# Moving the start addresses of the wide products' operands to multiples of 256 bytes in a partition

## The chip, the core and the metric

The kernel runs on one core of a Trainium2 chip. The metric is the device time of one execution in microseconds. Before the change the median of 3 runs is 2291.79 us (2289.28 to 2292.4). In the text TensorE is PE, its weight loads are PEld, VectorE is DVE, ScalarE is ACT, GpSimd is POOL and SyncE is SP.

## What is computed

A network of four layers on 256 tokens of 1024 features. Each layer is a half-weighted SwiGLU feed-forward block, a mixer, and a second feed-forward block, each added to the running `x` after an RMS norm:

```python
for i in range(DEPTH):
    x = x + 0.5 * _swiglu(_rms(x, norm_g[i, 0]), ffn_w_gate[i, 0], ffn_w_up[i, 0], ffn_w_down[i, 0])
    h = _rms(x, norm_g[i, 1])
    y = mixer[i](h)            # S5, HGRN2, gated delta net, MoBA attention
    x = x + y
    x = x + 0.5 * _swiglu(_rms(x, norm_g[i, 2]), ffn_w_gate[i, 1], ffn_w_up[i, 1], ffn_w_down[i, 1])
return _rms(x, final_norm_g)
```

A feed-forward block has two matrices of 1024x2816 and one of 2816x1024 in float32. There are eight such blocks, and the mixers have their own projections of 1024 to 2048, 4096, 6176 and 3072 columns and back.

## The kernel before

**Products in three passes.** All weights are float32 in HBM. `Weights._load` brings 128x1024 elements (512 KB) into a `raw` tile; `pump` makes `hi`, a rounded copy in the type fp32r, on ACT (L88), and `lo`, the rest, on DVE (L91; on POOL for every second unit of the delta net). The activations are split in the same way into a hi and a lo half, which stand side by side in one tile. A product is then hi x hi, hi x lo and lo x hi, three matmuls of type fp32r.

**The wide products** are in `Model.wide` (L347 to L349). The weights stream past (the moving operand, 128x512, from `hi` or `lo`), and a 128x128 piece of the activations is loaded into the array (the stationary operand). The tiles that give the stationary operand are `xhl` (the normed `x`, for up and gate projections and mixers), `hhl` (the hidden layer of a feed-forward block, for its down projection), `yhl`, `o` and `go` (the outputs of the mixers):

```python
ah, al = [a[:, k + j, m, t * 128:t * 128 + 128] for m in range(2)]
mm(p, ah, hi[:, j], start=first and j == 0, stop=False)
mm(p, ah, lo[:, j], start=False, stop=False)
mm(p, al, hi[:, j], start=False, stop=last and j == n - 1)
```

Each matmul has a weight load of its own. There are 2464 such triples, 7392 matmuls.

**The column products** are in `mm3` (L315 to L317), for those projections of the mixers whose result is wanted turned. The roles are changed there: 128x128 pieces of `hi` and `lo` are loaded, and 256 columns of `xhl` stream. There are 520 triples, 1560 matmuls.

**What sets the order.** Every engine's program is written out in full by the kernel's Python code, in the order of the blocks in `PARTS`; `take` and `pump` keep four units of weights split ahead of PE and four `raw` tiles loaded ahead. SP issues the loads of the weights.

**Where tiles start.** Tiles of a pool lie one behind the other in a partition, each begun at a multiple of 32 bytes, and the pools lie in the order in which `Model.__init__` opens them: `const`, `xp`, `small`, `work`, `raw`, `split`, then the pools of the single blocks. Within the tiles all operands of the two products are taken at steps of 512 bytes, so an operand's start, modulo 256, is that of its tile. Worked out from the tiles' sizes, the starts modulo 256 bytes are, before and after the change:

| operand | before | after | matmuls |
| --- | --- | --- | --- |
| wide, moving: `hi`, `lo` | 224 | 0 | 7392 |
| wide, stationary: `xhl` | 64 | 0 | 4704 |
| wide, stationary: `hhl` of the 8 feed-forward blocks in order | 128, 224, 192, 224, 64, 224, 224, 224 | 192, then 0 seven times | 8 x 264 |
| wide, stationary: `yhl` (S5), `go` (delta net), `o` (MoBA) | 224 | 0 | 192, 192, 96 |
| wide, stationary: `o` (HGRN2) | 192 | 0 | 96 |
| columns, moving: `xhl` | 64 | 0 | 1560 |
| columns, stationary: `hi`, `lo` | 224 | 0 | 1560 |

`raw` goes from 224 to 0 too. Before, `gains` (448 bytes), `hg_b` (132), `s5place` (32), `gd_w` (516) and `half_r` (8) are the tiles with sizes that are no multiple of 256 ahead of operands in their pools.

Of the kernel before, what the change touches and what calls it, by code (L numbers as in the profile page):

```python
# [9 lines left out]
F32 = mybir.dt.float32  # L10
# [17 lines left out]
def as_ap(ap, offset, dims):  # L28
    return bass.AP(tensor=ap.tensor, offset=ap.offset + offset, ap=dims)


class Weights:
# [6 lines left out]
    def __init__(self, nc, raw, split):  # L39
        self.nc, self.raw, self.split = nc, raw, split  # L40
        self.blocks, self.units = [], []
        self.loaded = self.ready = self.taken = 0
        self.tiles, self.parts = {}, {}
        self.aside = set()
# [59 lines left out]
class Model:  # L104
    def __init__(self, ctx, tc, I, out, parts):
        self.tc, self.nc, self.I, self.out = tc, tc.nc, I, out
        nc = self.nc
        self.const = ctx.enter_context(tc.tile_pool(name="const", bufs=1))
        self.xp = ctx.enter_context(tc.tile_pool(name="xp", bufs=1))
        self.small = ctx.enter_context(tc.tile_pool(name="small", bufs=2))  # L110
        self.work = ctx.enter_context(tc.tile_pool(name="work", bufs=2))
        raw = ctx.enter_context(tc.tile_pool(name="raw", bufs=Weights.RAW))
        split = ctx.enter_context(tc.tile_pool(name="split", bufs=Weights.HL))
        self.acc = ctx.enter_context(tc.tile_pool(name="acc", bufs=4, space=PSUM))
        self.dram = ctx.enter_context(tc.tile_pool(name="dram", bufs=1, space=bass.MemoryType.DRAM))
        self.w = Weights(nc, raw, split)
        self.parts = parts
        self.beside = []
        for p in parts:
            getattr(self, "plan_" + p[0])(*p[1:])  # L120
        with self.banks():
            self.start()
        self.prep = self.ahead = None
        self.bias = self.moba_bias if any(a[0] == "moba" for a in parts) else None
        with ExitStack() as early:
            for n, p in enumerate(parts):
                nxt = parts[n + 1] if n + 1 < len(parts) else None
                if n == 0 and any(a[0] == "s5" for a in parts):
                    self.s5_gain = self.gain_of([a for a in parts if a[0] == "s5"][0])
                    self.s5_pool = early.enter_context(tc.tile_pool(name="s5prep", bufs=1))  # L130
                    self.s5_u = self.s5_pool.tile([128, KT, 2, 8, 16], F32, name="s5u", tag="s5u")
                    self.prep = self.s5_prep(self.s5_pool)
                self.next_gain = self.gain_of(nxt)
                self.for_s5 = nxt is not None and nxt[0] == "s5"
                if nxt is not None and nxt[0] in ("hgrn", "gdn"):
                    made = early.enter_context(ExitStack())
                    pool = made.enter_context(tc.tile_pool(name="made", bufs=1))
                    self.ahead = lambda: getattr(self, nxt[0] + "_consts")(pool, *nxt[1:])
                aux = early.enter_context(ExitStack())
                aux.enter_context(self.banks(1 if p[0] == "gdn" else 4))  # L140
                self.due = p[0] in ("hgrn", "gdn", "moba")
                if p[0] != "s5":
                    self.r_col = self.norm_col()
                if p[0] == "s5":
                    self.settle(self.prep)
                    self.prep = None
                if nxt is None:
                    self.end = aux.enter_context(self.tc.tile_pool(name="last", bufs=1))
                    self.fin = self.end.tile([128, D], F32, name="fin")
                    nc.scalar.dma_start(self.fin, as_ap(I["final_norm_g"], 0, [[0, 128], [1, D]]))  # L150
                getattr(self, p[0])(*p[1:])
                aux.close()
                if p[0] in ("hgrn", "gdn") and n:
                    made.close()
                if p[0] == "s5":
                    early.close()
# [14 lines left out]
    def start(self):  # L171
        nc, I = self.nc, self.I
        c = self.const
        x = I["x"]

        self.x = self.xp.tile([128, 2, D], F32, name="x")
        rows = self.work.tile([128, 128], F32, name="rows", bufs=1)
        nc.sync.dma_start(rows[:96], as_ap(I["norm_g"], 0, [[128, 96], [1, 128]]))
        for c0 in range(0, D, 512):
            nc.sync.dma_start(self.x[:, :, c0:c0 + 512], as_ap(x, c0, [[D, 128], [128 * D, 2], [1, 512]]))  # L180
        nc.scalar.dma_start(rows[96:104], as_ap(I["final_norm_g"], 0, [[128, 8], [1, 128]]))
        nc.scalar.dma_start(rows[104:112], as_ap(I["s5_d"], 0, [[128, 8], [1, 128]]))
        self.ident = c.tile([128, 128], F32, name="ident")
        nc.gpsimd.memset(self.ident, 0.0)
        nc.gpsimd.affine_select(out=self.ident, in_=self.ident, compare_op=OP.not_equal, fill=1.0,
                                base=0, pattern=[[-1, 128]], channel_multiplier=1)
        self.zero = c.tile([128, 512], mybir.dt.bfloat16, name="zero")
        nc.vector.memset(self.zero, 0.0)
        self.gains = c.tile([128, 112], F32, name="gains")
        p = self.aux.tile([128, 512], F32, name="aux")  # L190
        nc.tensor.transpose(p[:, :112], rows[:112], self.ident[:112, :112])
        nc.scalar.copy(self.gains, p[:, :112])
        self.next_gain = self.gain_of(self.parts[0])
        self.r_row = self.xp.tile([128, L], F32, name="r_row")
        self.for_s5 = False
        self.begin_x()
        self.w.pump(1, self.tc.keep_in_program_order)
        for cc in range(2):
            for t in range(2):
                self.turn_x(t, cc)  # L200
            self.w.pump(2 + cc, self.tc.keep_in_program_order)
        for cc in range(2):
            for t in range(2):
                self.square_x(t, cc)
# [383 lines left out]
    def s5_prep(self, pool):  # L588


        nc, I = self.nc, self.I
# [16 lines left out]
        p = self.aux.tile([128, 512], F32, name="aux")  # L608
# [8 lines left out]
        for src, first, second, signs in ((b_in, b1, b2, (1, 1, -1, 1)), (c_in, c1, c2, (1, -1, -1, -1))):  # L617
            for h0 in (0, 8):
                p = self.aux.tile([128, 512], F32, name="aux")
# [93 lines left out]
        split = lambda a: a.rearrange("p g (t h) -> p g t h", h=16)  # L713
# [5 lines left out]
        for sign, base in ((1, 0), (-1, 7)):  # L719
            nc.gpsimd.affine_select(out=self.s5_at, in_=self.s5_at, compare_op=OP.is_ge, fill=0.0, base=base,  # L720
                                    pattern=[[128 * sign, 2], [0, 4], [-8 * sign, 32]], channel_multiplier=sign)
        self.s5_place = pool.tile([128, 8], F32, name="s5place")
        v.tensor_reduce(self.s5_place, self.ident.rearrange("p (a t) -> p t a", t=8), op=OP.add, axis=mybir.AxisListType.X)
        for j in range(8):
            r = slice(8 * j, 8 * j + 8)
# [17 lines left out]
            p = self.aux.tile([128, 512], F32, name="aux")  # L743
# [13 lines left out]
            for h, eb in zip(rs, ebs):  # L757
                p = self.aux.tile([128, 512], F32, name="aux")
# [265 lines left out]
    def hgrn_consts(self, pool, i):  # L1024

        nc = self.nc
# [4 lines left out]
        nc.gpsimd.dma_start(rows[32:33], as_ap(self.I["hg_norm_g"], 0, [[128, 1], [1, 128]]))  # L1031
        p = self.aux.tile([128, 512], F32, name="aux")
        nc.tensor.transpose(p[:, :33], rows[:33], self.ident[:33, :33])
        b = pool.tile([128, 33], F32, name="hg_b")
        nc.vector.tensor_copy(b, p[:, :33])
        c = pool.tile([128, 3, 8], F32, name="hg_c")
        m = pool.tile([128, 3, 8], F32, name="hg_m")
        nc.vector.tensor_tensor(m[:, 0], b[:, 0:8], b[:, 8:16], op=OP.max)
# [228 lines left out]
    def gdn_consts(self, pool, i):  # L1267
        nc, I = self.nc, self.I
# [4 lines left out]
        p = self.aux.tile([128, 512], F32, name="aux")  # L1273
        nc.tensor.transpose(p[:, :128], rows[:, 0], self.ident)
        nc.tensor.transpose(p[:, 128:129], rows[:1, 1], self.ident[:1, :1])
        self.gd_w = pool.tile([128, 129], F32, name="gd_w")
        nc.vector.tensor_copy(self.gd_w, p[:, :129])
        self.gd_ab = pool.tile([128, 2, 16], F32, name="gd_ab")
        nc.gpsimd.dma_start(self.gd_ab[:, 0], as_ap(I["gdn_a_log"], 0, [[0, 128], [1, 16]]))
        nc.gpsimd.dma_start(self.gd_ab[:, 1], as_ap(I["gdn_dt_bias"], 0, [[0, 128], [1, 16]]))  # L1280
# [20 lines left out]
        for n in range(5):  # L1301
            a = pool.tile([128, 2, 32], I32, name="gd_a")
            b = pool.tile([128, 3, 32], F32, name="gd_b")
# [8 lines left out]
        b = pool.tile([128, 2, 32], F32, name="gd_c")  # L1312
# [13 lines left out]
    def gdn(self, i):  # L1326
        nc = self.nc
        F16 = mybir.dt.float16
        mm = nc.tensor.matmul
        with ExitStack() as ctx:  # L1330
            pool = ctx.enter_context(self.tc.tile_pool(name="gdn", bufs=1))
# [115 lines left out]

                self.proj_cols(4, v_done)

            half_r = pool.tile([128, 2], F32, name="half_r")  # L1450
            nc.vector.tensor_scalar(half_r, self.r_col, 0.5, None, op0=OP.mult)

            def gate(z):
# [371 lines left out]
```

## Time and profile before

| what | value |
| --- | --- |
| median of 3 runs | 2291.79 us |
| the profiled execution | 2291.63 us |
| its span, first to last instruction | 2289.8 us |
| granted TensorE clock, mean | 0.983 |
| PE busy | 2177.5 us (95%) |
| PEld busy | 1774.8 us (78%) |
| DVE busy | 1460.9 us (64%) |
| ACT busy | 1159.5 us (51%) |
| POOL busy | 286.8 us (13%) |
| HBM read | 375.65 MB, 169 GB/s with the writes, over the span |

A busy PE is not a PE at its peak: matmuls overlap, and a matmul of 0.39 us may be followed by the next after 0.23 us. What such a stream costs is therefore read from the distance between starts, or from a stretch's length over the number of matmuls in it, and not from the mean duration. The chain of work that ended last tells which engine's work the end of the program hung on, and for how much of the span.

### The profile page before, as it was taken

What the parts mean: (1) busy time and instruction counts of PE and PEld (TensorE: products, weight loads), DVE (VectorE), ACT (ScalarE), POOL (GpSimd) and SP (SyncE); (2) the same over time, 40 slices, a digit from 0 to 9 for tenths busy, and PEclk for the clock granted to TensorE, in tenths of its full rate; (3) what the DMA queues carried; (4) which work ended last, traced back from release to release, by engine and by line L of the source; (5) the groups of instructions that cost most, each with busy time, mean ns of one, the idle gap of its engine ahead of it and who ended that gap; (6) DMA issues with size and microseconds to landing.
All of it is one profiled execution on the core that took longest, in us unless ns stands there. A gap on an engine that the chain in (4) does not pass through costs nothing.

```text
span 2289.8 us, 30309 instructions
## 1 busy us (share of the span) xinstructions
PE 2177.5 (95%) x11480; PEld 1774.8 (78%) x11480; DVE 1460.9 (64%) x2412; ACT 1159.5 (51%) x1876; POOL 286.8 (13%) x305
## 2 busy tenths in 40 slices
PE   8979788999999999999999888899999999999998
PEld 6767566888888887887888766777788888898886
DVE  7886664556555866556555788977655555666555
ACT  6434344445444755445444567765544444545443
POOL 0597600000000000001000322222000000000000
PEclk9999989999999999999999999999999999999999
DMA  8655966655555644555654532333555655655553
GB/s 251 192 190 200 225 180 158 197 177 191 179 177 178 186 146 150 182 175 175 185 183 161 171 102 86 99 111 114 181 181 169 200 177 173 204 166 175 183 169 108
DMA packets 317906, 389.63 MB, mean 170 GB/s; under 512 B 14192, under 2 KB 247856, under 8 KB 316736
## 3 DMA queue, kind: packets, MB, share of 16 engines
q1 hardware_dynamic: 314768, 383.92, 53.9%
q10 hardware_dynamic: 2800, 3.68, 0.9%
q8 instruction: 90, 1.47, 0.3%
q14 instruction: 56, 0.46, 0.1%
q0 software_dynamic: 192, 0.10, 0.0%
HBM read 375.65 MB, written 12.01 MB: 169 GB/s over the span
## 4 chain that ended last, share of the span: by engine, by line
PE 81%; DVE 9%; ACT 3%; DMA 3%; POOL 2%; issue 1%; SPq 0%; ACTq 0%; DVEq 0%; POOLq 0%
PE acc L348 23%; PE acc L349 23%; PE acc L347 23%; DVE lo L91 2%; PE acc L316 2%; PE acc L315 2%; PE acc L317 2%; PE aux L439 2%; DVE cy L1395 1%; DMA raw<-in_ffn_w_up_dram 1%; ACT hi L88 1%; PE aux L230 1%; DMA tab<-s_k 1%; POOL s5e L734 1%; POOL s5e L733 1%
## 5 line engine op out<-in xcount | busy, mean ns | idle before, releaser
L91 DVE TENSOR_TENSOR lo<-raw,hi 128x1024 fp32r<-128x1024 f32 x648 | 809.8, 1251 | 614.1 <-ACT hi L88 613.1
L88 ACT CAST hi<-raw 128x1024 fp32r<-128x1024 f32 x681 | 712.5, 1048 | 734.2 <-PE acc L349 680.9
L347 PE MATMUL acc<-hi,xhl 128*128 128x512 f32 x1568 | 635.0, 405 | 10.4 <-ACT hi L88 9.6
L348 PE MATMUL acc<-lo,xhl 128*128 128x512 f32 x1568 | 627.9, 400 | 2.4 <-DVE lo L91 2.3
L349 PE MATMUL acc<-hi,xhl 128*128 128x512 f32 x1568 | 626.4, 400 | 0.0
L347 PEld LDWEIGHTS acc<-hi,xhl 128*128 128x128 f32 x1568 | 298.2, 190 | 81.0 <-ACT hi L88 10.5
L349 PEld LDWEIGHTS acc<-hi,xhl 128*128 128x128 f32 x1568 | 297.9, 190 | 73.9 <-issue 2.7
L348 PEld LDWEIGHTS acc<-lo,xhl 128*128 128x128 f32 x1568 | 298.2, 190 | 72.4 <-DVE lo L91 4.9
L349 PE MATMUL acc<-hi,hhl 128*128 128x512 f32 x704 | 278.0, 395 | 0.0
L347 PE MATMUL acc<-hi,hhl 128*128 128x512 f32 x704 | 277.9, 395 | 0.0
L348 PE MATMUL acc<-lo,hhl 128*128 128x512 f32 x704 | 277.0, 393 | 0.0
L348 PEld LDWEIGHTS acc<-lo,hhl 128*128 128x128 f32 x704 | 133.0, 189 | 29.1
L347 PEld LDWEIGHTS acc<-hi,hhl 128*128 128x128 f32 x704 | 132.9, 189 | 28.8
L349 PEld LDWEIGHTS acc<-hi,hhl 128*128 128x128 f32 x704 | 132.8, 189 | 28.7
L317 PE MATMUL acc<-xhl,lo 128*128 128x256 f32 x520 | 149.5, 289 | 0.0
L316 PE MATMUL acc<-xhl,hi 128*128 128x256 f32 x520 | 148.8, 288 | 0.3 <-DVE xhl L241 0.3
L315 PE MATMUL acc<-xhl,hi 128*128 128x256 f32 x520 | 148.9, 289 | 0.1
L427 ACT ACTIVATE sl<-acc,norm_r 128x256 f32<-128x256 f32 x176 | 83.7, 475 | 110.9 <-PE acc L349 95.9
L91 POOL TENSOR_TENSOR lo<-raw,hi 128x1024 fp32r<-128x1024 f32 x33 | 81.5, 2470 | 349.8 <-ACT hi L88 329.7
L430 DVE TENSOR_TENSOR h<-acc,sl 128x256 f32<-128x256 f32 x176 | 73.9, 420 | 54.9 <-ACT sl L427 54.9
L315 PEld LDWEIGHTS acc<-xhl,hi 128*128 128x128 f32 x520 | 98.1, 190 | 2.6 <-issue 1.7
L316 PEld LDWEIGHTS acc<-xhl,hi 128*128 128x128 f32 x520 | 98.5, 190 | 1.6 <-issue 0.9
(564 smaller groups left out, 2281.8 us busy)
## 6 DMA issues: line engine op xcount, KB each, us to landing
raw<-in_ffn_w_gate_dram SPq DMA_DIRECT2D x174, 512.0 KB, 4.0
raw<-in_ffn_w_up_dram SPq DMA_DIRECT2D x174, 512.0 KB, 5.1
raw<-in_ffn_w_down_dram SPq DMA_DIRECT2D x80, 1024.0 KB, 5.0
raw<-in_gdn_w_in_dram SPq DMA_DIRECT2D x24, 1024.0 KB, 5.4
raw<-in_hg_w_in_dram SPq DMA_DIRECT2D x16, 1024.0 KB, 5.4
raw<-in_moba_w_in_dram SPq DMA_DIRECT2D x12, 1024.0 KB, 5.6
raw<-in_ffn_w_down_dram SPq DMA_DIRECT2D x16, 512.0 KB, 3.6
raw<-in_s_w_glu_dram SPq DMA_DIRECT2D x16, 512.0 KB, 4.5
```

The lines of the kernel that those rows point to most:

```text
L88: pin(self.nc.scalar.copy(hi, src))
L91: eng.tensor_tensor(lo, src, hi.bitcast(F32), op=OP.subtract)
L230: nc.tensor.transpose(q[:, j * 128:j * 128 + 128], self.x[:, t, k * 128:k * 128 + 128], self.ident)
L315: t.matmul(p, hi, ah, start=first, stop=False)
L316: t.matmul(p, hi, al, start=False, stop=False)
L317: t.matmul(p, lo, ah, start=False, stop=last)
L347: mm(p, ah, hi[:, j], start=first and j == 0, stop=False)
L348: mm(p, ah, lo[:, j], start=False, stop=False)
L349: mm(p, al, hi[:, j], start=False, stop=last and j == n - 1)
L427: nc.scalar.activation(sl, p[:, :256], AF.Silu, scale=self.r_col[:, t:t + 1])
L430: return nc.vector.tensor_tensor(waiting[-1][1][:, t], p[:, 256:], sl, op=OP.mult)
L439: nc.tensor.transpose(q[:, c:c + 128], h[:, t, f * 128:f * 128 + 128], self.ident)
```

## The change

Three pools are opened in another order: `xp` behind `small` and `work`, and `split` ahead of `raw`. Five tiles get unused columns, and the instructions go on using the columns that they used. No instruction is added, taken out or put elsewhere: on each engine the same instructions stand in the same order, and only their addresses differ.

```diff
         self.const = ctx.enter_context(tc.tile_pool(name="const", bufs=1))
-        self.xp = ctx.enter_context(tc.tile_pool(name="xp", bufs=1))
         self.small = ctx.enter_context(tc.tile_pool(name="small", bufs=2))
         self.work = ctx.enter_context(tc.tile_pool(name="work", bufs=2))
+        self.xp = ctx.enter_context(tc.tile_pool(name="xp", bufs=1))
+        split = ctx.enter_context(tc.tile_pool(name="split", bufs=Weights.HL))
         raw = ctx.enter_context(tc.tile_pool(name="raw", bufs=Weights.RAW))
-        split = ctx.enter_context(tc.tile_pool(name="split", bufs=Weights.HL))
...
-        self.gains = c.tile([128, 112], F32, name="gains")
+        self.gains = c.tile([128, 120], F32, name="gains")
...
-        nc.scalar.copy(self.gains, p[:, :112])
+        nc.scalar.copy(self.gains[:, :112], p[:, :112])
...
-        self.s5_place = pool.tile([128, 8], F32, name="s5place")
+        self.s5_place = pool.tile([128, 16], F32, name="s5place")[:, :8]
...
-        b = pool.tile([128, 33], F32, name="hg_b")
-        nc.vector.tensor_copy(b, p[:, :33])
+        b = pool.tile([128, 41], F32, name="hg_b")
+        nc.vector.tensor_copy(b[:, :33], p[:, :33])
...
-        self.gd_w = pool.tile([128, 129], F32, name="gd_w")
-        nc.vector.tensor_copy(self.gd_w, p[:, :129])
+        self.gd_w = pool.tile([128, 169], F32, name="gd_w")
+        nc.vector.tensor_copy(self.gd_w[:, :129], p[:, :129])
...
-            half_r = pool.tile([128, 2], F32, name="half_r")
+            half_r = pool.tile([128, 26], F32, name="half_r")[:, :2]
```

## Rows read from the trace of the kernel before

**Rows 1.** The page: PE's busy time, and the chain by engine and line.
```profile
PE 2177.5 (95%) x11480; PEld 1774.8 (78%) x11480; DVE 1460.9 (64%) x2412; ACT 1159.5 (51%) x1876; POOL 286.8 (13%) x305
...
PE 81%; DVE 9%; ACT 3%; DMA 3%; POOL 2%; issue 1%; SPq 0%; ACTq 0%; DVEq 0%; POOLq 0%
...
by line: PE acc L348 22.9%; PE acc L349 22.9%; PE acc L347 22.8%; DVE lo L91 1.9%; PE acc L316 1.6%; PE acc L315 1.6%; PE acc L317 1.6%; PE aux L439 1.6%; DVE cy L1395 1.4%; issue 1.3%; DMA raw<-in_ffn_w_up_dram 1.3%; ACT hi L88 0.9%; PE au
```

**Rows 2.** Groups of matmuls: xcount, busy us, mean ns, idle us before them.
```profile
L347 PE MATMUL acc<-hi,xhl 128*128 128x512 f32 x1568 | 635.0, 405 | 10.4 <-ACT hi L88 9.6
...
L347 PE MATMUL acc<-hi,hhl 128*128 128x512 f32 x704 | 277.9, 395 | 0.0
...
L315 PE MATMUL acc<-xhl,hi 128*128 128x256 f32 x520 | 148.9, 289 | 0.1
...
L349 PE MATMUL acc<-hi,go 128*128 128x512 f32 x64 | 26.1, 410 | 0.0
...
L349 PE MATMUL acc<-hi,o 128*128 128x512 f32 x64 | 25.8, 403 | 0.0
...
L349 PE MATMUL acc<-hi,yhl 128*128 128x512 f32 x64 | 24.5, 393 | 0.0
```

**Rows 3.** Four unbroken stretches with hhl: length, PE, PEld, DVE, ACT busy, clock, DMA.
```profile
494.46:521.70 27.24, 27.24 (x122) 22.52 (x120) 0.68 (x1) 0.58 (x1) 1.00 0.58 193
685.21:713.21 28.00, 28.00 (x122) 22.49 (x120) 0.68 (x1) 0.58 (x1) 1.00 0.57 194
1208.82:1236.94 28.12, 28.12 (x122) 22.60 (x120) 0.68 (x1) 0.58 (x1) 1.00 0.57 191
216.85:242.05 25.20, 25.20 (x110) 20.27 (x108) 0.00 (x0) 0.00 (x0) 1.00 0.84 289
```

**Rows 4.** PE in order of time, with xhl: start us, duration us, instruction.
```profile
609.89 0.40 PE L347 MATMUL acc<-hi,xhl 128*128 128x512 f32 x1
609.89 0.19 PEld L348 LDWEIGHTS acc<-lo,xhl 128*128 128x128 f32 x1
...
611.53 0.40 PE L348 MATMUL acc<-lo,xhl 128*128 128x512 f32 x1
```

**Rows 5.** The same view: bf16 matmuls at full clock, and fp32r ones at half.
```profile
252.31 3.18 PE L253 MATMUL aux<-zero 128*128 128x512 bf16 x14
...
149.34 0.63 PE L348 MATMUL acc<-lo,xhl 128*128 128x512 f32 x1
...
151.05 0.60 PE L349 MATMUL acc<-hi,xhl 128*128 128x512 f32 x1
```

**Rows 6.** The same view: column products, and transposes behind them.
```profile
2009.90 0.29 PE L315 MATMUL acc<-xhl,hi 128*128 128x256 f32 x1
...
2010.62 0.29 PE L315 MATMUL acc<-xhl,hi 128*128 128x256 f32 x1
...
2011.34 0.27 PE L1765 MATMUL aux<-ident,e 128*128 128x128 f32 x1
...
2011.56 0.27 PE L1767 MATMUL aux<-ident,e 128*128 128x128 f32 x1
```

**Rows 7.** Stretches: all engines (PE, PEld, DVE, ACT, POOL), then L347 alone (PE, PEld).
```profile
0.00:250.00 250.00, 224.65 (x1099) 175.57 (x1099) 189.65 (x320) 123.77 (x196) 139.60 (x154) 0.97 0.70 221
...
1250.00:1600.00 350.00, 308.44 (x2257) 254.58 (x2256) 280.76 (x575) 212.95 (x463) 101.18 (x49) 0.97 0.36 114
...
0.00:250.00 250.00, 108.42 (x264) 51.18 (x264) 0.97 0.70 221
...
1250.00:1600.00 350.00, 62.35 (x149) 29.61 (x149) 0.97 0.36 114
```

**Rows 8.** Groups of instructions that make hi and lo.
```profile
L91 DVE TENSOR_TENSOR lo<-raw,hi 128x1024 fp32r<-128x1024 f32 x648 | 809.8, 1251 | 614.1 <-ACT hi L88 613.1
L88 ACT CAST hi<-raw 128x1024 fp32r<-128x1024 f32 x681 | 712.5, 1048 | 734.2 <-PE acc L349 680.9
```

## The prediction

> **What bounds the kernel now.** I read the chain of waits first. PE holds 81% of it, and the three lines of the wide products alone 22.8 + 22.9 + 22.9 = 68.6% of the span, 1571 us; the three lines of the column products hold 1.6% each, together 4.8% or 110 us [rows 1]. The rest is spread over DVE, ACT, DMA and POOL. So the question is what one matmul of these two streams costs. The change adds and moves no instruction; it can only act through addresses, and most of all here.
>
> The mean duration doesn't tell that cost, since a matmul of 0.39 us overlaps the next. I take stretches in which nothing breaks the stream and divide by the number of weight loads, one per matmul. With `hhl` as the stationary operand there are four [rows 3]: 27.24 us / 120 = **227.0 ns** a matmul in the second feed-forward block, 28.00 / 120 = 233.3 in the third, 28.12 / 120 = 234.3 in the fifth, 25.20 / 108 = 233.3 in the first. Instruction, shape, engine and granted clock (1.00) are the same. What differs is where `hhl` starts, modulo 256: at 224, 192, 64 and 128. The weights that stream past start at 224 in all four. So the address counts, and the stream is fastest where both operands start alike. With `xhl`, at 64, seven starts cover 611.53 - 609.89 = 1.64 us, 234.3 ns each [rows 4], as for `hhl` at 64.
>
> What does such a stream cost without a penalty? 14 bf16 matmuls of the same 512 columns take 3.18 us; without the last one's 0.38 us of duration, 2.80 / 13 = **215.5 ns** [rows 5]. At the clock's upper level, 2.4 GHz, 512 columns are 213.3 ns. At the lower level, 1.2 GHz, four fp32r matmuls with their operands at 224 and 64 start within 151.05 - 149.34 = 1.71 us, 427 ns each [rows 5], and 512 / 1.2 is 426.7: no penalty is seen there. So the addresses cost something only where 4-byte columns are read at the full rate, 12 to 19 ns a matmul.
>
> The column products, with a stream of 256 columns from 64, take (2010.62 - 2009.90) / 6 = 120 ns [rows 6], where 256 columns at 2.4 GHz are 106.7. The transposes, whose loads are of the same size and follow each other directly, start every (2011.56 - 2011.34) / 2 = 110 ns [rows 6].
>
> **What a start at 0 should cost.** No row shows a moving operand at a multiple of 256, so the price has to be bounded. From below: 215.5 ns, the row without penalty. From above: the dearest pitch seen, 234.3, plus a penalty unit if both reads at 0 disturb each other (a rival, below). Between them one pattern decides for me. The excess over pure streaming is 227.0 - 213.3 = 13.7 ns with 2048 bytes read from 224, and 120 - 106.7 = 13.3 ns with 1024 bytes read from 64. Both are the time of 32 columns, 128 bytes (32 / 2.4 = 13.3 ns). A cost by the byte would halve with the shorter stream; this one doesn't, so it looks like one more unit of 128 bytes touched per matmul, because neither 224 nor 64 is a multiple of 128. At 0 that unit falls away. This is worked out from three rows and not shown by one; still I take 215.5 ns for wide products with both operands at 0. For the column products I take 109 to 110 ns, the transposes' pitch, since the load becomes the limit.
>
> **The sum at full rate**, with counts from [rows 2] (three lines each) and starts from the table:
> - `xhl`, 4704 matmuls: 234.3 - 215.5 = 18.8 ns, 88.4 us.
> - `hhl` at 224, five blocks, 1320: 11.5 ns, 15.2 us.
> - `hhl` at 192 and 64, 528: 18.3 ns, 9.7 us.
> - `hhl` of the first block goes from 128 to 192, not to 0: 264 at no change, 0 us (bounds: 17.8 ns each way, 4.7 us).
> - `yhl`, `go` and MoBA's `o`, at 224, 480: 11.5 ns, 5.5 us; HGRN2's `o`, at 192, 96: 17.8 ns, 1.7 us.
> - column products, 1560: 120 - 109 = 11 ns, 17.2 us.
>
> That is 120.5 us of wide and 17.2 us of column products. Not all of it reaches the end. By these pitches the wide products are 4704 x 234.3 + 1320 x 227.0 + 264 x (233.3 + 234.3 + 233.3) + 480 x 227.0 + 96 x 233.3 ns = 1718 us of stream, of which 1571 us are on the chain, 91%; the column products are 1560 x 120 ns = 187 us, of which 110 us are, 59%. So 110 + 10 = 120 us are saved on the chain.
>
> A faster PE then waits where it was just ahead. In the first 250 us DVE is busy 190 us, beside POOL with 140, and between 1250 and 1600 us DVE is busy 281 of 350 us [rows 7]; there the recurrences of S5 and the delta net feed PE. These stretches hold (264 + 149) x 3 wide matmuls [rows 7], 975 without the first block's `hhl`: 975 x 18.8 ns x 91% = 17 us. I let half of it be eaten there, 8 us. In the other stretches ACT and DVE need 1.05 and 1.25 us per unit of weights [rows 8], and twelve matmuls read it, 12 x 215.5 ns = 2.6 us; so neither becomes the bound. The DMA share of 0.57 in [rows 3] would rise by the pitch, 234 / 215.5, to 0.62, with room left. Gain: **112 us**.
>
> ACT's and DVE's operands move too, all from 224 to 0, and no row shows them elsewhere. They hold 0.9% and 1.9% of the chain [rows 1], 64 us; a tenth of it either way is 6 us, and I take 0. The loads' landing places move with `raw`; weights are 1.3% of the chain in one wait (30 us), and I take 0 there as well, with 3 us either way.
>
> The profiled execution took 2291.63 us, 0.16 below the median, so the sum needs no correction: 2291.6 - 112 = **2180 us**.
>
> **Rivals.**
> *Only equal starts count.* Then `xhl` and the odd `hhl` fall to 227.0 and nothing below it: 4704 x 7.3 + 528 x 6.8 + 96 x 6.3 ns = 38.5 us, of which 91% are 35 us, **2256 us**; the columns add 0 to 10 us. For it: 227.0 is the lowest pitch that any fp32r row has, and equal starts give it. Against it: the equal excess of both shapes, and that equality can't explain why columns with unequal starts pay exactly one unit. [...]
>
> *Both reads at 0 collide: slower.* A load starts in the same hundredth of a microsecond as the matmul beside it [rows 4]. With both at a 256-byte boundary they could ask for the same place at once, at the price of one more unit: 227.0 + 13.3 = 240.3 ns. Then `xhl` loses 6.0 ns x 4704 = 28 us, what stood at 224 loses 13.3 x 1800 = 24 us, the rest 7 x 624 = 4 us, 56 us in all, 51 on the chain, and the columns 13.3 x 1560 x 59% = 12 us: **2355 us**. It decides from a mean pitch above 234 ns. Against it: of the rows at hand, the equal starts are the fastest and not the slowest.
>
> *Addresses don't do it.* The 7 ns could hang on something that goes with the block and not with the start; then nothing changes, **2292 us**. Against it: `hhl` at 224 and 64 differ at the same clock and the same DMA share [rows 3]. [...]
>
> **How the numbers follow.** Forecast 0.58; only equal starts 0.25; a pitch between these two, some 2215 us, 0.05; no effect 0.05; collision 0.07. Two runs of this kernel can be told apart from about 0.2%, 5 us. Faster is 0.58 + 0.25 + 0.05 = 0.88, same 0.05, slower 0.07. The forecast's own range is 2150 (the whole 137.7 us, and 4 us for ACT, DVE and the loads) to 2205. To leave out no more than 2 in 10 the range must take in the first rival: 2150 to 2260.
>
> **What would show it.** Right: wide stretches with 120 loads in 25.9 us, the same for `xhl` and `hhl`; a column pitch below 112 ns; the first block's down projection still near 233; a larger share of DVE in the chain. Wrong: 227 in every stretch (equal starts), 240 (collision), or 234 beside 227 as now. If the pitch falls to 215.5 and the time by less than 80 us, the step on the chain is wrong, and the waits for `hi` and `lo` must have grown.

## The result and the profile after

The changed kernel takes 2254.39 us (median of 4 runs, 2251.23 to 2255.48), the kernel before, beside it, 2292.1 us. The ratio is 0.9834, with a 95% interval of 0.9817 to 0.9851: faster by 37.7 us or 1.7%. The forecast was 2180 us; the time lies in the range given and almost on the first rival, "only equal starts count" (2256 us).

The page of the changed kernel, and the line of its chain by program lines (against [rows 1]):

```profile
PE 2147.5 (95%) x11480; PEld 1771.5 (79%) x11480; DVE 1464.5 (65%) x2412; ACT 1159.8 (51%) x1876; POOL 288.1 (13%) x305
...
L91 DVE TENSOR_TENSOR lo<-raw,hi 128x1024 fp32r<-128x1024 f32 x648 | 813.1, 1257 | 585.4 <-ACT hi L88 582.3
L88 ACT CAST hi<-raw 128x1024 fp32r<-128x1024 f32 x681 | 713.1, 1049 | 708.2 <-PE acc L349 657.5
```

```profile
by line: PE acc L349 22.6%; PE acc L347 22.6%; PE acc L348 22.6%; DVE lo L91 2.0%; PE acc L315 1.7%; PE acc L316 1.7%; PE acc L317 1.7%; PE aux L439 1.6%; issue 1.5%; DVE cy L1395 1.4%; DMA raw<-in_ffn_w_up_dram 1.2%; ACT hi L88 1.0%; PE au
```

The same instructions run, and ACT and DVE need as long for `hi` and `lo` as before (1049 and 1257 ns, against 1048 and 1251 in [rows 8]). The three lines of the wide products now hold 67.8% of 2253.7 us, 1528 us, against 1571: 43 us less.

The stretches that answer to [rows 3], in the same order of columns: the first, second, third and fifth feed-forward block's down projection.

```profile
214.43:239.17 24.74, 24.74 (x110) 20.29 (x108) 0.00 (x0) 0.00 (x0) 1.00 0.82 286
483.64:510.89 27.25, 27.25 (x122) 22.53 (x120) 0.68 (x1) 0.58 (x1) 1.00 0.59 193
671.00:698.24 27.24, 27.24 (x121) 22.53 (x120) 0.68 (x1) 0.58 (x1) 1.00 0.59 195
1182.16:1209.38 27.22, 27.22 (x121) 22.53 (x120) 0.68 (x1) 0.58 (x1) 1.00 0.58 195
```

With 120 loads they last 27.22 to 27.25 us, 227 ns a matmul, in the blocks that had 227.0, 233.3 and 234.3 before. What was at 227 stayed there; nothing fell to 25.9 us. The first block, whose `hhl` went to 192 and not to 0, has 24.74 / 108 = 229.1 ns, against 233.3. PE in order of time, with `xhl` and in the column products (against [rows 4] and [rows 6]):

```profile
609.68 0.39 PE L347 MATMUL acc<-hi,xhl 128*128 128x512 f32 x1
...
611.72 0.39 PE L347 MATMUL acc<-hi,xhl 128*128 128x512 f32 x1
...
1954.74 0.28 PE L315 MATMUL acc<-xhl,hi 128*128 128x256 f32 x1
...
1955.46 0.28 PE L315 MATMUL acc<-xhl,hi 128*128 128x256 f32 x1
```

Nine starts with `xhl` cover 2.04 us, 226.7 ns each, where it was 234.3. Six in the column products cover 0.72 us, 120 ns each, as before.

So the gain comes, stretch by stretch, from where wide products with unequal starts ran. The lead of one stretch is known to 1 or 2 us only, since falls of the granted clock lie elsewhere in each execution: the stretch from PE's 4000th to its 4500th matmul ran at a mean granted clock of 0.98 before and 1.00 after, and among the variants below in which all its starts are equal it took 84.9 to 85.0 us at 1.00 and 86.2 to 86.5 at 0.98. The stretch of the delta net gave nothing: between PE's 6000th and 8500th matmul the lead over the kernel before shrinks from 28.0 to 27.1 us. Column products, whose pitch didn't change, and recurrences on DVE (busy 316 of the 405 us) fill much of it; which of the two held the gain back was not tried. One part doesn't belong to the product streams: between PE's 1000th and 1500th matmul, in S5, 4.0 us are gained. There PE waits for tables of weights from DRAM (rows of 512 bytes, `tab`). The DMA issues of the kernel before, then of the changed one (count, KB each, median us from issue to landing), and PE's waits in the same order (total us, times, longest):

```profile
tab<-s_k SPq DMA_DIRECT2D x32, 128.0 KB, 8.8
```

```profile
tab<-s_k SPq DMA_DIRECT2D x32, 128.0 KB, 6.6
```

```profile
PE acc L882 <- DMA tab<-s_k: 17.3, 3, 6.3
```

```profile
PE acc L882 <- DMA tab<-s_k: 11.6, 3, 5.0
```

The chain that ended last runs through these loads. Its pieces there, start and length in us, before, then after:

```profile
263.49 13.54 DMA tab<-s_out
277.04 8.59 DMA tab<-s_k
285.65 8.22 DMA tab<-s_k
```

```profile
262.55 11.75 DMA tab<-s_out
274.32 6.32 DMA tab<-s_k
280.65 6.06 DMA tab<-s_k
```

In sum 30.4 us became 24.1. The whole stretch, before and after (the last three figures are the granted clock, the DMA share and GB/s):

```profile
226.41:298.83 72.42, 50.74 (x501) 36.28 (x500) 46.67 (x72) 19.25 (x33) 40.44 (x73) 0.86 1.03 235
```

```profile
223.83:292.23 68.40, 52.95 (x502) 37.28 (x501) 46.98 (x72) 19.17 (x33) 40.58 (x73) 0.83 0.97 253
```

The DMA engines are busy all through it (shares of 1.03 and 0.97), and move more in the same time after the change (253 GB/s against 235). `tab` started at 224 modulo 256 before and starts at 0 now.

### The profile page after: what moved, and what is told of

The parts are those of the page before. It is cut to its first block, busy times and chain, and to the rows that moved or that the text cites. A ratio compares the mean times of both kernels' runs of the same rounds, so it can differ in the third digit from the quotient of the medians.

```text
span 2253.7 us, 30309 instructions
## 1 busy us (share of the span) xinstructions
PE 2147.5 (95%) x11480; PEld 1771.5 (79%) x11480; DVE 1464.5 (65%) x2412; ACT 1159.8 (51%) x1876; POOL 288.1 (13%) x305
## 4 chain that ended last, share of the span: by engine, by line
PE 80%; DVE 9%; ACT 4%; DMA 3%; POOL 2%; issue 1%; SPq 0%; ACTq 0%; DVEq 0%; POOLq 0%
PE acc L349 23%; PE acc L347 23%; PE acc L348 23%; DVE lo L91 2%; PE acc L315 2%; PE acc L316 2%; PE acc L317 2%; PE aux L439 2%; DVE cy L1395 1%; DMA raw<-in_ffn_w_up_dram 1%; ACT hi L88 1%; PE aux L230 1%; POOL s5e L733 1%; POOL s5e L734 1%; POOL s5tmp L732 1%
## 5 line engine op out<-in xcount | busy, mean ns | idle before, releaser
L91 DVE TENSOR_TENSOR lo<-raw,hi 128x1024 fp32r<-128x1024 f32 x648 | 813.1, 1257 | 585.4 <-ACT hi L88 582.3
L88 ACT CAST hi<-raw 128x1024 fp32r<-128x1024 f32 x681 | 713.1, 1049 | 708.2 <-PE acc L349 657.5
L347 PE MATMUL acc<-hi,xhl 128*128 128x512 f32 x1568 | 627.2, 400 | 9.9 <-ACT hi L88 9.4
L348 PE MATMUL acc<-lo,xhl 128*128 128x512 f32 x1568 | 618.9, 395 | 2.8 <-DVE lo L91 2.7
L349 PE MATMUL acc<-hi,xhl 128*128 128x512 f32 x1568 | 616.9, 394 | 0.0
L347 PEld LDWEIGHTS acc<-hi,xhl 128*128 128x128 f32 x1568 | 297.1, 190 | 73.0 <-ACT hi L88 10.7
L347 PE MATMUL acc<-hi,hhl 128*128 128x512 f32 x704 | 276.9, 393 | 0.0
L347 PEld LDWEIGHTS acc<-hi,hhl 128*128 128x128 f32 x704 | 132.7, 188 | 27.0
```

The lines of the kernel that those rows point to most:

```text
L88: pin(self.nc.scalar.copy(hi, src))
L91: eng.tensor_tensor(lo, src, hi.bitcast(F32), op=OP.subtract)
```

## The experiments

All of them are variants of the changed kernel. Theory A is that equal starts alone count, theory B that both must be multiples of 256, theory C that their difference must be a multiple of 256. Ratios are against the kernel before on the same chip.

### Bursts of matmuls at chosen starts

```diff
+            for n, (so, mo, w, c) in enumerate(self.GROUPS):
+                for _ in range(24 if n == 0 else 6):
+                    keep(mm(z, self.zero[:, :128], self.zero, start=True, stop=True))
+                for _ in range(33):
+                    keep(mm(p[:w, :c], stat[:, so // 4:so // 4 + w], mov[:, mo // 4:mo // 4 + c], start=True, stop=True))
```

`stat` and `mov` begin at multiples of 256, so `so` and `mo` are the starts of the loaded and of the streamed operand; `w` and `c` are their columns. The data are copies of the last `x`.

> The changed kernel, with 25 bursts of 33 fp32r matmuls added behind its last product; each burst has its own starts of the stationary and the moving operand within a partition (0 to 256 bytes), some a narrower load or a shorter stream; their results are not used. Theory A (only the difference of the two starts counts): equal starts give 227 ns a matmul at 0, 32, 64, 128 and 224 alike; differences of 32, 96, 160 and 224 give 233 to 234; 192 gives 228 to 229, as the first block's down projection shows in the changed kernel. Theory B (both must begin at multiples of 256): 227 at 0 and 0 alone, 233 or more for equal starts at 32. Theory C (the difference must be a multiple of 256): differences of 64 and 128 give 233 as 32 does; by theory A in its narrow form (differences that are multiples of 64 are good) they give 227 to 229. On the rest of 12 ns above the bf16 pitch of 215.5: if the load's reads cause it, a load of 64 or 32 columns brings the pitch at 0 and 0 down to 216 to 221; if it belongs to each fp32r matmul, it stays 227 there, and streams of 384 and 256 columns give 173 and 120 (13.3 ns above pure streaming each).

The table gives the mean distance of the last 24 starts of each burst, in ns; the first few of a burst are further apart (the first seven starts of the burst 240 - 0 cover 1.80 us, 257 ns each, where its last ones are at 226.7). (The first burst, at 0 and 0, is left out; it is in the second set.)

| load's start - stream's start, stream 128x512 | ns |
| --- | --- |
| 32 - 0, 64 - 0, 96 - 0, 128 - 0 | 233.3, 233.3, 234.2, 232.1 |
| 160 - 0, 192 - 0, 224 - 0, 256 - 0 | 233.3, 228.9, 233.3, 227.1 |
| 32 - 32, 64 - 64, 128 - 128, 224 - 224 | 226.7, 227.1, 226.7, 226.7 |
| 0 - 224, 64 - 224, 96 - 224, 128 - 224, 192 - 224 | 233.3, 234.2, 232.8, 233.6, 233.3 |
| 0 - 0, load of 64 and of 32 columns | 230.0, 231.7 |
| 0 - 0, stream of 384, 256, 128 columns | 173.3, 120.0, 111.7 |
| 224 - 64, stream of 256 columns | 120.0 |

PE in order of time shows it as bursts: start, length in us, and 33 matmuls. At 32 - 0, 64 - 0, then 192 - 0, 224 - 0, 32 - 32 and 64 - 64:

```profile
2266.93 8.06 PE L177 MATMUL aux<-mov,stat 128*128 128x512 f32 x33
...
2275.95 8.05 PE L177 MATMUL aux<-mov,stat 128*128 128x512 f32 x33
...
2311.97 7.92 PE L177 MATMUL aux<-mov,stat 128*128 128x512 f32 x33
...
2320.85 8.06 PE L177 MATMUL aux<-mov,stat 128*128 128x512 f32 x33
...
2329.86 7.84 PE L177 MATMUL aux<-mov,stat 128*128 128x512 f32 x33
...
2338.67 7.87 PE L177 MATMUL aux<-mov,stat 128*128 128x512 f32 x33
```

Equal starts last 7.84 to 7.87 us, the unequal ones shown 8.05 to 8.06, and 192 - 0 lies between. The bursts give back the kernels' pitches to within 0.5 ns: 224 - 224 and 64, 128, 192 - 224 those of [rows 3], 192 - 0 that of the first block now. B falls: 32 - 32 is as good as 0 - 0 (226.7 ns against 226.8). A's narrow form (any difference that is a multiple of 64) falls: 64 - 0 and 128 - 0 are as bad as 32 - 0 (233.3 and 232.1 ns against 233.3). C holds but for 192 - 0. Pure streaming is 0.417 ns a column by these bursts: from 512 (226.8) to 384 (173.3) and to 256 columns (120.0) the pitch falls by 53.5 and 53.3 ns, 128 columns each, which is 2.4 columns a ns; the prediction's 2.4 GHz are this rate, and its 1.2 GHz the rate of 512 columns in 427 ns [rows 5], where the granted clock was 0.50 (149.00 to 151.30 us of the kernel before). With a load of 128 columns and equal starts, the 13.3 ns above it are the same with 512, 384 and 256 columns, and with 512 they are the same at all five starts tried. With 256 columns, unequal starts cost nothing: 224 - 64 and 0 - 0 both give 120.0. A narrower load makes the pitch of a 512-column stream worse instead of better (230.0 and 231.7 ns against 226.8). With a stream of 256 columns it is the other way: at 0 - 0 a load of 32 columns gives 113.3 ns, 6.7 above pure streaming.

### Equal starts that are no multiples of 256, in the whole kernel

```diff
+        c.tile([128, 8], F32, name="pad")
         self.ident = c.tile([128, 128], F32, name="ident")
```

> The changed kernel with every tile 32 bytes later: both operands start at 32 modulo 256, equal and no multiple of 256. Theory A (equal starts count): 227 ns a matmul and the time of the changed kernel, 2254 us, ratio to before 0.983. Theory B (multiples of 256 count): 233 to 234 ns in all stretches, 2285 us or more, ratio 0.997 or more.

Measured: 2262.62 us, ratio 0.9878 (0.9863 to 0.9893). PE with `xhl`:

```profile
619.61 0.39 PE L348 MATMUL acc<-hi,xhl 128*128 128x512 f32 x1
...
621.88 0.39 PE L349 MATMUL acc<-lo,xhl 128*128 128x512 f32 x1
```

Ten starts in 2.27 us are 227 ns, so A is right on the streams. The time is 8 us above the changed kernel, though, and outside its interval. Matmul by matmul against the changed kernel, 3.5 of the 5.3 us between the two profiled executions arise between PE's 1000th and 1500th, in S5. Another 1.5 and 1.4 arise from the 4000th and from the 5000th, where the granted clock was 0.98 and 0.99 and not 1.00. In the feed-forward stretches at clock 1.00 it is 0.0. Two more shifts, with the changed kernel on the same chip, ask what this is.

> The changed kernel with every tile 64 bytes later, so that both operands start at 64 modulo 256. If equality is all that counts, 227 ns in every stretch and the time of the changed kernel within 0.2%. If the 8 us by which the shift of 32 bytes was slower than the changed kernel belong to the start itself (a boundary of 64 bytes is missed at 32), they are gone here; if they belong to anything but a multiple of 256, they are here again (2260 to 2264 us).

> The changed kernel with every tile 128 bytes later, both operands at 128 modulo 256. The same question as for 64 bytes: equality alone gives 227 ns and the time of the changed kernel within 0.2%; a wish for multiples of 256 outside PE gives 2260 to 2264 us.

> The changed kernel as it stands, on the chip of the two shifted ones: 2252 to 2256 us, ratio 0.983.

Measured: 2261.92 us (0.9874, 0.9858 to 0.9891) at 64, 2257.73 (0.9856, 0.9842 to 0.9871) at 128, and 2255.63 (0.9848, 0.9834 to 0.9863) for the changed kernel. The shift of 128 is within the 0.2% that equality alone would allow. The intervals overlap, so the times alone leave the ranking open. They also go with the mean granted clock of the single runs: at 0.984 the changed kernel took 2251 to 2255 us over its two sets of runs, the shift of 128 2255.5 and 2257.0, and that of 64 2257.8; the shift of 32 had no run above 0.982, so part of its 8 us may be the clock. In the traces, though, the shifts of 64 and 128 lose 2.7 and 4.9 us in the same stretch of S5, where the second execution of the changed kernel gains 0.6 on the first. With the shift of 128 the tables land thus:

```profile
tab<-s_k SPq DMA_DIRECT2D x32, 128.0 KB, 8.7
```

In 8.7 us, as before the change (8.8). In the second execution of the changed kernel it was 7.3. So something outside PE seems to ask for a multiple of 256.

### The tables of S5 alone

```diff
+                    self.s5_pool.tile([128, 8], F32, name="pad")
                     self.s5_u = self.s5_pool.tile([128, KT, 2, 8, 16], F32, name="s5u", tag="s5u")
...
-        self.s5_place = pool.tile([128, 16], F32, name="s5place")[:, :8]
+        self.s5_place = pool.tile([128, 16 + 56], F32, name="s5place")[:, :8]
```

> The changed kernel with the tiles of the S5 preparation alone 32 bytes later (tab, into which the tables are loaded in rows of 512 bytes, starts at 32 instead of 0); xhl, hhl, hi, lo and raw stay where they are, yhl moves with tab. If the place where the tables' loads land costs 4 us in S5: the loads of tab from s_k land in 8.4 to 8.8 us instead of 6.6 to 7.3, PE's waits for them grow from 12 to 13 us to 15 to 17, and with yhl's 192 matmuls at 233 ns (1.2 us) the time is 2259 to 2261 us. If not: 2255 to 2257 us.

Measured: 2259.03 us, ratio 0.9859 (0.9842 to 0.9875). Landing, and PE's waits:

```profile
tab<-s_k SPq DMA_DIRECT2D x32, 128.0 KB, 8.4
```

```profile
PE acc L883 <- DMA tab<-s_k: 15.5, 3, 6.1
```

Both lie where the expectation put them. Matmul by matmul, 4.7 us are lost in that stretch of S5, and 1.3 in the next, which holds `yhl`'s products. The stretch of S5, as above:

```profile
224.30:297.35 73.05, 53.77 (x501) 37.73 (x500) 47.38 (x72) 19.17 (x33) 41.01 (x74) 0.79 1.01 231
```

The DMA engines moved 231 GB/s, and in the executions with `tab` at 224, 32, 64 and 128 229 to 237, against 246 to 253 in all those with `tab` at 0. The granted clock was 0.79 here and 0.83 in the changed kernel, so some of the 4.7 us can be the clock. The kernel before, at 0.86, was 4.0 us longer in this stretch than the changed one all the same. The time itself is 4 us above that of the variant of the last experiment, on the same chip, with intervals that overlap, so the trace carries this verdict. The other tiles of the S5 preparation moved with `tab`; that the loads are what counts rests on their landing and on PE's waits for them.

### xhl alone off the weights' start

```diff
         self.r_row = self.xp.tile([128, L], F32, name="r_row")
+        self.xp.tile([128, 16], F32, name="pad")
...
         self.begin_x()
+        self.xp.tile([128, 48], F32, name="pad2")
```

> The changed kernel with xhl alone 64 bytes later; the weights and the other activations stay at 0. Theory A in its narrow form (differences that are multiples of 64 are as good as equal): 227 to 229 ns with xhl, 2254 to 2262 us. Theory C (the difference must be a multiple of 256): 233 to 234 ns with xhl, 4704 x 6.5 ns, 91% of it on the chain, 28 us: 2282 us.

> The changed kernel with xhl alone 32 bytes later; the weights and the other activations stay at 0. Theories A, B and C: 233 to 234 ns with xhl, 227 with hhl, 2280 to 2285 us. If the pitch with xhl stays 227, what made xhl slow before was not its start against that of the weights.

Measured: 2274.16 us (0.9926, 0.9909 to 0.9942) at 64, 2276.84 (0.9941, 0.9927 to 0.9956) at 32. PE with `xhl` at 64, then in the other kernel at 32:

```profile
618.43 0.39 PE L350 MATMUL acc<-lo,xhl 128*128 128x512 f32 x1
...
619.83 0.40 PE L350 MATMUL acc<-lo,xhl 128*128 128x512 f32 x1
```

```profile
617.65 0.40 PE L350 MATMUL acc<-lo,xhl 128*128 128x512 f32 x1
...
618.35 0.40 PE L350 MATMUL acc<-lo,xhl 128*128 128x512 f32 x1
```

Six starts in 1.40 us and three in 0.70, 233.3 ns in both. (One more tile, `s5x` of S5, lies beside `xhl` and moved with it.) Undoing this one pair of starts gives back 20 to 22 us of the 37.7 by the medians, and 21 to 25 by the ratios to the kernel before (the changed kernel was not run beside these two); at full rate it would be 4704 x 6.5 ns = 31 us, so 65 to 80% of it reaches the end, less than the 91% of the prediction (82% once half of its 975 matmuls in S5 and the delta net is taken off). It also misses my forecasts, which were 2254 to 2262 by theory A and 2282 by theory C at 64, and 2280 to 2285 at 32.

### Is any pair of starts better than 227 ns?

> The changed kernel with 24 bursts of 33 fp32r matmuls behind its last product, results not used. Differences of the starts of 4, 8, 16, 48, 80, 112, 144, 176, 208 and 240 bytes: if only equality is good, all give 231 to 235 ns but the smallest, which may still give 227; if some difference lets the two reads interleave, one of them falls towards 216. Loads 4, 12, 28 and 60 KB away, equal modulo 256: 227 each if distance does not count. Streams of 508, 496, 480, 448 and 320 columns with equal starts: with a fixed price per matmul, columns / 2.4 + 13.3 ns, that is 225.0, 220.0, 213.3, 200.0 and 146.7; if the pitch is rounded up to whole units of 13.3 ns beyond a smaller price, 226.7, 226.7, 213.3, 200.0 and 146.7. Equal starts at 16 and at 4 bytes: 227. Loads of 64 columns with differences of 64 and 128: 230 to 233.

The edit is that of the first set of bursts, with other starts.

| load's start - stream's start, stream 128x512 | ns |
| --- | --- |
| 0 - 0 | 226.8 |
| 4 - 0, 8 - 0, 16 - 0, 48 - 0, 80 - 0 | 232.2, 230.5, 233.3, 233.3, 232.1 |
| 112 - 0, 144 - 0, 176 - 0, 208 - 0, 240 - 0 | 233.3, 233.3, 230.0, 233.3, 226.7 |
| 4, 12, 28, 60 KB - 0 | 227.1 each |
| 16 - 16, 4 - 4 | 233.3, 237.8 |
| 64 - 0, 128 - 0, load of 64 columns | 232.8, 229.4 |
| 0 - 0, stream of 508, 496, 480, 448, 320 columns | 227.4, 223.3, 216.7, 202.8, 146.7 |

The bursts 16 - 0, 240 - 0, 4 KB - 0, 16 - 16 and 4 - 4:

```profile
2287.03 8.05 PE L178 MATMUL aux<-mov,stat 128*128 128x512 f32 x33
...
2349.95 7.86 PE L178 MATMUL aux<-mov,stat 128*128 128x512 f32 x33
...
2358.77 7.88 PE L178 MATMUL aux<-mov,stat 128*128 128x512 f32 x33
...
2434.24 8.04 PE L178 MATMUL aux<-mov,stat 128*128 128x512 f32 x33
...
2443.25 8.19 PE L178 MATMUL aux<-mov,stat 128*128 128x512 f32 x33
```

None of the pairs tried goes below 226.7. Distance doesn't count: 4 to 60 KB apart it is 227.1 ns. A load at 240 with the stream at 0 (16 bytes short of equal, modulo 256) is as good as an equal start (226.7), and equality alone isn't enough either: at 16 - 16 and 4 - 4 it costs as much as a bad difference, or more (233.3 and 237.8). Of the starts at multiples of 32, where all tiles of this kernel lie, equal ones are the best with 512 columns (226.7 to 227.1 ns), as theory A has it; 192 - 0 (228.9) comes within about 2 ns. Of the two guesses on the stream's length neither fits: 320 columns (and 384 and 256 above) pay 13.3 ns, 508, 496, 480 and 448 columns 15.7 to 16.7.

### The first block's hhl at 0 too

```diff
-        self.s5_place = pool.tile([128, 16], F32, name="s5place")[:, :8]
+        self.s5_place = pool.tile([128, 32], F32, name="s5place")[:, :8]
```

> The changed kernel with hhl of the first feed-forward block at 0 too (s5place 64 bytes wider). By the bursts, its 264 matmuls go from 228.7 to 226.7 ns: 0.5 us, not measurable, 2254 to 2256 us; in the trace its down projection has starts 226.7 ns apart.

Measured: 2254.85 us, ratio 0.9843 (0.9829 to 0.9858): not to be told from the changed kernel, as expected. In the first block's down projection:

```profile
224.74 0.39 PE L347 MATMUL acc<-hi,hhl 128*128 128x512 f32 x1
...
226.78 0.39 PE L347 MATMUL acc<-hi,hhl 128*128 128x512 f32 x1
```

Nine starts in 2.04 us, 226.7 ns.

## Why the prediction was wrong

**What held.** The bound was read rightly: PE's stream of wide products, where 7 ns a matmul came out for most of them. That the address does it, that the streams' pitch is the figure to look at, and that ACT and DVE stay as they are, was right as well. So was the count of work on which the sum stood.

**The step that failed** is the one headed "What a start at 0 should cost". It took the 13.3 ns above pure streaming for one more unit of 128 bytes touched, "because neither 224 nor 64 is a multiple of 128. At 0 that unit falls away", and so put 215.5 ns for wide products and 109 for columns. The pattern was real: 13.3 ns whether 2048 or 1024 bytes are read. But it was a price that an fp32r matmul of 512 columns with a full load pays at least, at every start tried. At 0 - 0 it is still there, with 512, 384 and 256 columns (226.7 to 227, 173.3, 120.0). A fixed price and a price for a partial unit give the same figures in the rows of before, since every stream there started off a multiple of 128 (224 or 64); I took the one that promised more. The row of 215.5 ns was one of bf16 matmuls, and no fp32r row of 512 columns stood below 227.0.

By its own terms, with the pitches measured since: `xhl` 4704 x (234.3 - 226.9) = 34.8 us and not 88.4; `hhl` at 224, `yhl`, `go` and MoBA's `o` nothing and not 20.7; the odd `hhl` 528 x 6.8 = 3.6 and not 9.7; the first block 264 x (233.3 - 229.1) = 1.1 and not 0; HGRN2's `o` 0.6 and not 1.7; the columns nothing and not 17.2. That is 40 us at full rate in place of 137.7.

**Smaller ones.** Of these 40 us, 37.7 less the 4 us of S5, 34 us, reached the end. The prediction's own step from streams to the end, with these pitches, gives 91% of 40 us less half of 975 x 7.4 ns x 91%, that is 33 us: it held. The delta net kept its part altogether, as the rows of DVE there had warned; the 8 us that I let be eaten were the right place. The loads' landing places, which I took at 0 with 3 us either way, gave about 4 us in S5, where rows of 512 bytes land. The weights' loads, which the prediction had named, showed little: they are off the chain as before, but for one long wait at `raw` (1.2% of the chain, 1.3% before).

**The rivals.** "Only equal starts" gave 2256 us for what became 2254.4. That it comes so close is partly luck: it expected 35 us from the streams and they gave 34, and the tables, which it didn't have, gave 4 more. In the bursts, moving the load's start alone from 0 to 32, with the stream at 0, takes the pitch from 226.8 to 233.3 ns. "Both reads at 0 collide" (240.3 ns) and "addresses don't do it" are out by the same two figures.

On the landing of the loads the runs show times alone: `tab<-s_k` took 6.6 to 7.3 us with `tab` at 0 and 8.4 to 8.8 us with it at 32, 64, 128 and 224. What makes the difference was not measured.

**What stays open.** Why a stream whose two operands start alike is faster (226.7 to 227.1 ns, against 228.9 to 234.2 at the other multiples of 32), why 240 - 0 is as good (226.7) and 192 - 0 nearly so (228.9), and what the 13.3 ns are: the bursts rule out the distance and, among equal starts at multiples of 32 bytes, the start. They don't rule out the load: with 256 columns a load of 32 columns halves the excess (6.7 ns, against 13.3), and the bf16 row, with an excess of 2 ns (215.5 against 213.3), had loads of 98 ns at the median, where the fp32r ones of [rows 3] took 188 (22.52 us / 120). The type, the 4 bytes a column and the load weren't separated further. The starts of bf16 operands, or of fp32r ones at half the clock (0.50 granted), weren't varied either, so the prediction's sentence that addresses cost something only where 4-byte columns are read at the full rate stays unshown. Whether the rows' length matters to the loads of the tables is open too: `tab<-s_out`, with rows of 8192 bytes in the same queue, fell from 9.2 to 7.3 us as well, and `tab<-s_in`, with rows as long, did not (9.9, then 11.7).

## What to carry to other kernels

When a stream of matmuls runs at different pitches in places that differ in nothing but the tile, compare the tiles' starts; in such a stream of fp32r with 512 columns, put both operands at the same multiple of 32 bytes within 256 (here 226.7 to 227.1 ns against 228.9 to 234.2), and where the program waits for loads of 512-byte rows, try letting them land at multiples of 256 (here 6.6 to 7.3 us against 8.4 to 8.8). An excess that is the same in all rows at hand may be a fixed price: before counting on its vanishing, look for one row without it on the same instruction and type, and if there is none, measure a burst of 33 matmuls first.

## What the runs showed that was not expected

- An fp32r matmul with a load of 128 columns costs 0.417 ns a column and 13.3 ns on top at its best for streams of 256, 320, 384 and 512 columns (120.0, 146.7, 173.3 and 226.7 ns); bf16 ones with 512 columns 215.5. With 512 columns, unequal starts add 2 to 8 ns more (240 - 0 nothing); with 256 the one pair tried added nothing.
- A narrower load makes a stream of 512 columns slower: 230.0 ns with 64 columns and 231.7 with 32, against 226.8 with 128, at equal starts. With a stream of 256 columns it is the other way: 113.3 ns with a load of 32 columns, 120.0 with 128.
- Streams a little shorter than 512 columns save less than they leave out: 508 columns take 227.4 ns, 512 take 226.8.
- Loads of 128 KB in rows of 512 bytes that land at a multiple of 256 bytes arrive in 6.6 to 7.3 us (median of 32) instead of 8.4 to 8.8, on a wait that was 15.5 to 17.3 us of PE and is 11.6 to 13.2 at 0.
